# The first products of a two-layer decoder trunk: unnormed tokens, constant transposes ahead, and two widths in turn

## The chip, the cores and the metric

The kernel runs as one program on one core of one Trainium2 chip. The metric is the device time of one execution in microseconds. Engines are named as in the profile: PE is TensorE (PEld its weight loads), DVE is VectorE, ACT is ScalarE, POOL is GpSimd, SP is SyncE, which here only issues DMAs.

## The reference

The input x is one batch of 256 tokens by 1024 channels in float32. Two layers each do three steps: half a SwiGLU, a mixer, half a SwiGLU.

```python
def rms_norm(x, g):
    y = xf * lax.rsqrt(jnp.mean(xf * xf, axis=-1, keepdims=True) + EPS)
    return (y * g).astype(x.dtype)

def swiglu(h, w_gate, w_up, w_down):
    return (jax.nn.silu(h @ w_gate) * (h @ w_up)) @ w_down

for layer in range(2):
    x = x + 0.5 * swiglu(rms_norm(x, pre_norm[layer]), pre_w_gate[layer], pre_w_up[layer], pre_w_down[layer])
    h = rms_norm(x, mix_norm[layer])
    x = x + mixer(h)          # layer 0: SSD and MLA heads; layer 1: window attention and GLA heads
    x = x + 0.5 * swiglu(rms_norm(x, post_norm[layer]), post_w_gate[layer], post_w_up[layer], post_w_down[layer])
```

The hidden width of a SwiGLU is 2816, that is 22 blocks of 128. The change touches the four SwiGLU steps (called `ffn`) and the start of the program.

## The kernel before

**Two parts for each number.** Every float32 operand of a product is split in a high part (`wh`, `hT` at index 0, `acth`) and a low part (`wl`, index 1, `actl`). ACT casts the high part, DVE subtracts it from the source to get the low part. A product of two operands is then three products on PE: high by high, low by high, high by low.

**Weights.** `Stream.load` takes pieces of the packed weights in the order of use. Each piece (128 by 1024, 512 KB) is one DMA on SP's queue (line 73), one ACT cast (line 77) and one DVE subtraction (line 78). There are four raw buffers and eight pairs of `wh` and `wl`, so SP waits for DVE to free a raw buffer, and ACT and DVE wait for PE to free a pair.

**Norm.** `norm` squares and sums a tile of 128 tokens on ACT (line 245), takes the power −1/2 on POOL (line 229), multiplies by the factor and the gain on DVE (line 253, the tile `h`), transposes the eight 128 by 128 blocks on PE (`m_nrm`, line 117), and splits them into `hT` (lines 224 and 225). `hT` is four tiles, each with two of the eight channel blocks k, both parts and both token tiles t.

**A SwiGLU.** The first `G0` = 4 of the 22 blocks go with tokens as rows: `in_tok` (lines 272 to 274) makes 24 products of 512 columns for the gate (`p_g`) of token tile 0, 24 for up (`p_u`) of tile 0, then the same for tile 1; each pair is evicted (lines 359 and 360) and turned back by four transposes (`m_ffT`). The other 18 blocks f go with channels as rows: `in_ch2` makes, for each k, one product of 512 columns (`wh` by both parts of both token tiles, line 300) and one of 256 columns (`wl` by the high part, line 301). The down products (`proj`, lines 316 to 318) follow.

**The start.** x of tile 0 goes on SP's queue ahead of the weights, the gain on ACT's, the constants (`sq`, which holds the identity for the transposes) and x of tile 1 on POOL's. The other constants come in `constants_more`, on POOL's queue too, from 17 us on.

**The order of the work.** The program is not run in the order of the code: a scheduler places the instructions of each engine in a list by a timeline of its own, and each engine then works through its list from the front, waiting at each instruction for what that one needs. What is changed in the code can so move rows on every engine.

Of the kernel before, what the change touches and what calls it, by code (L numbers as in the profile page):

```python
# [15 lines left out]
P = 128  # L16
# [40 lines left out]
class Stream:  # L57
# [10 lines left out]
    def load(self, widths):  # L68
        nc = self.nc
        res = []  # L70
        for i, x in enumerate(widths):
            raw = self.pool.tile([P, x], F32, tag="raw", name=f"raw{self.n}_{i}", bufs=self.raw_bufs)
            nc.sync.dma_start(out=raw, in_=self.flat[self.off:self.off + P * x].rearrange("(p w) -> p w", w=x))
# [10 lines left out]
class Net:  # L84
# [38 lines left out]


    POOLS = {"a": (("a4", 4096, 9),), "b": (("b1", 1024, 2), ("b2", 2048, 4), ("b4", 4096, 13))}

    def constants(self):
        nc, a = self.nc, self.args
        self.sq = self.sb.tile([P, 3 * P], F32, tag="sq", name="sq", bufs=1)
        nc.gpsimd.dma_start(out=self.sq, in_=a["sq"])  # L130
        self.ident = self.sq[:, SQ["ident"]]
        self.mhalf = self.small([P, 8], "mhalf")
        nc.gpsimd.memset(self.mhalf, -0.5)

    def constants_more(self):
        nc, a = self.nc, self.args
        self.row = self.sb.tile([P, ROW_N], F32, tag="row", name="row", bufs=1)
        nc.gpsimd.dma_start(out=self.row, in_=a["row"].partition_broadcast(P))
        self.conv = self.small([P, 16, 5], "conv")
        nc.gpsimd.dma_start(out=self.conv, in_=a["conv"])  # L140
        kq = self.small([96, 2], "kq")
        nc.gpsimd.dma_start(out=kq, in_=a["kq"])
        self.wg = self.small([17, 256], "wg")
        nc.gpsimd.dma_start(out=self.wg, in_=a["wg"])
        self.pcol = self.small([P, 2], "pcol", I32)
        nc.gpsimd.dma_start(out=self.pcol, in_=a["pos_col"])
        self.prow = self.blk([P, S], "prow", I32)
        nc.gpsimd.dma_start(out=self.prow, in_=a["pos"].partition_broadcast(P))
# [11 lines left out]
        nc.gpsimd.dma_start(out=out_, in_=a["outside"])  # L160
# [78 lines left out]
    def norm(self, x, t, g, hT):  # L239

        nc = self.nc
        ss = self.small([P, 4], "ss", bufs=2)
        junk = self.small([P, 512], "junk")
        for h in range(2):
            nc.scalar.activation(out=junk, in_=x[:, h * 512:(h + 1) * 512], func=AF.Square, scale=1.0 / 32,
                                 accum_out=ss[:, h:h + 1])
        nc.vector.tensor_scalar(out=ss[:, 2:3], in0=ss[:, 0:1], scalar1=ss[:, 1:2], scalar2=EPS, op0=ALU.add, op1=ALU.add)  # L247
        self.power(ss[:, 3:4], ss[:, 2:3])
        h_ = self.blk([P, D], "h")
        turned = []  # L250
        for h in range(2):
            s = slice(h * 512, (h + 1) * 512)
            nc.vector.scalar_tensor_tensor(out=h_[:, s], in0=x[:, s], scalar=ss[:, 3:4], in1=g[:, s], op0=ALU.mult, op1=ALU.mult)
# [10 lines left out]
    def mm_tok(self, out, at, ks, t, w, first, last):  # L264

        mm = self.nc.tensor.matmul
        c = slice(t * P, (t + 1) * P)
        for i, k in enumerate(ks):
            ah, al = at(k)
            ah, al = ah[:, c], al[:, c]  # L270
            wh, wl = w[i]
            mm(out, ah, wh, start=first and i == 0, stop=False)  # L272
            mm(out, al, wh, start=False, stop=False)  # L273
            mm(out, ah, wl, start=False, stop=last and i == len(ks) - 1)  # L274

    def in_tok(self, out, hT, t, w, n, per):

        for s, (hi, lo) in enumerate(w):
            ww = [(hi[:, j * n:(j + 1) * n], lo[:, j * n:(j + 1) * n]) for j in range(per)]
            self.mm_tok(out, lambda k: self.hk(hT, k), range(per * s, per * s + per), t, ww, s == 0, s == len(w) - 1)  # L280
# [12 lines left out]
    def in_ch2(self, out, hT, w):  # L293
# [54 lines left out]
    def ffn(self, hT, x, after):  # L348
# [3 lines left out]
        wg = [s for _ in range(2) for s in st.load([2 * n0, 2 * n0])]  # L352
        wu = [s for _ in range(2) for s in st.load([2 * n0, 2 * n0])]
        for t in range(2):
            pg, pu = self.bank([P, n0], "g"), self.bank([P, n0], "u")
            self.in_tok(pg, hT, t, wg, n0, 2)
            self.in_tok(pu, hT, t, wu, n0, 2)
            sg = self.blk([P, n0], "sg")
            nc.scalar.activation(out=sg, in_=pg, func=AF.Silu)
            nc.vector.tensor_tensor(out=sg, in0=sg, in1=pu, op=ALU.mult)  # L360
# [95 lines left out]
    def mixer0(self, hT, x, after):  # L456
# [53 lines left out]
        for t in range(2):  # L510
            qn = self.blk([P, 8, 96], "qnat", grp="a")
            qr = self.blk([P, 8, 2, 16], "qr")
            for j in range(2):
                b = self.bank([P, 4, 96], "qb")
                bf = b.rearrange("p a b -> p (a b)")
                for k in range(3):
                    self.mm_tok(bf, lambda k: (qaT[0][:, k, :], qaT[1][:, k, :]), [k], t,
# [18 lines left out]
        for t in range(2):  # L536
            if t == 1:
                xbc(13, BC[1][:, 1, :])
# [4 lines left out]
            for j in range(2):  # L543
                b = self.bank([P, 4, P], "kvb")
                bf = b.rearrange("p a b -> p (a b)")
                for k in range(2):
                    self.mm_tok(bf, lambda k: (kvT[:, 0, k, :], kvT[:, 1, k, :]), [k], t,
# [458 lines left out]
    def run(self, out, steps):  # L1006
        nc = self.nc
        x = [self.big.tile([P, D], F32, tag=f"x{t}", name=f"x{t}", bufs=1) for t in range(2)]
        nc.sync.dma_start(out=x[0], in_=self.args["x"][:P, :])
        g, hT = self.gain(steps[0][1], nc.scalar), self.new_hT()  # L1010
        self.constants()
        self.norm(x[0], 0, g, hT)
        with self.tc.issue_after(self.pow.ins):
            nc.gpsimd.dma_start(out=x[1], in_=self.args["x"][P:, :])
        self.norm(x[1], 1, g, hT)
        with self.tc.issue_after(self.pow.ins):
            self.constants_more()
        for i, (what, _) in enumerate(steps):
            hT = self.step(what, hT, x, steps[i + 1][1] if i + 1 < len(steps) else None, out)

# [131 lines left out]
```

## Time and profile before

| | |
|---|---|
| median of 3 runs | 1045.36 us (1044.97 to 1046.19) |
| the profiled execution's own time | 1044.57 us |
| its span | 1042.8 us |
| PE busy | 1017.3 us (98%), 5561 instructions |
| DVE busy | 686.2 us (66%) |
| ACT busy | 570.3 us (55%) |
| mean granted TensorE clock | 0.995 |

The span runs from the first instruction to the last; the execution's own time is 1.8 us longer. A matmul's recorded time overlaps that of the next, so the pitch of the products is read from start to start. PE is nearly always at work; what an edit is worth is read from whether PE starts earlier, waits somewhere, or has more or slower products.

### The profile page before, as it was taken

The numbers are of one execution on the slowest core, as the hardware profiler recorded it, in microseconds if no ns is written. First come the engines' busy times: TensorE is split into PE (matmuls) and PEld (weight loads), VectorE is DVE, ScalarE is ACT, GpSimd is POOL, SyncE is SP. The second block draws the span as 40 slices with busy tenths as digits, with TensorE's granted clock in tenths as the row PEclk, the third lists the DMA queues.
The fourth block names the chain that finished last, engine by engine and source line by source line (L and its number), as shares of the span: only waits on it lengthen the run. The fifth ranks groups of instructions, "written<-read, shape, count | busy, mean of one in ns | idle before, by whom it ended". The sixth has DMA issues, their size and how long they took to land.

```text
span 1042.8 us, 15030 instructions
## 1 busy us (share of the span) xinstructions
PE 1017.3 (98%) x5561; PEld 872.3 (84%) x5561; DVE 686.2 (66%) x1054; ACT 570.3 (55%) x1036; POOL 87.5 (8%) x110
## 2 busy tenths in 40 slices
PE   6999999989799999999999999999999999999998
PEld 5888888988798888888888888888887778888886
DVE  6876754588777567677545767654588576666541
ACT  5755543467857366655434655643465456555530
POOL 2200000106233200000000000000011200000000
PEclk9999999999999999999999999999999999999999
DMA  8866555364434457565564655555463345665451
GB/s 300 280 204 188 191 190 176 115 209 162 151 111 161 144 182 241 184 198 184 197 190 159 223 197 186 191 189 168 142 222 101 102 160 181 191 193 184 148 197 40
DMA packets 52089, 185.93 MB, mean 178 GB/s; under 512 B 5911, under 2 KB 5928, under 8 KB 52016
## 3 DMA queue, kind: packets, MB, share of 16 engines
q1 hardware_dynamic: 49248, 176.58, 52.1%
q0 software_dynamic: 2048, 6.83, 2.0%
q10 hardware_dynamic: 720, 1.57, 0.4%
q8 instruction: 43, 0.70, 0.3%
q14 instruction: 30, 0.25, 0.1%
HBM read 183.89 MB, written 1.06 MB: 177 GB/s over the span
## 4 chain that ended last, share of the span: by engine, by line
PE 95%; ACT 1%; DVE 1%; DMA 1%; issue 1%; POOL 0%; DVEq 0%; ACTq 0%; POOLq 0%
PE p_u L300 13%; PE p_g L300 13%; PE p_acc L316 9%; PE p_acc L318 9%; PE p_acc L317 9%; PE p_u L301 7%; PE p_g L301 7%; PE p_g L272 1%; PE p_g L273 1%; PE p_g L274 1%; PE p_u L274 1%; PE p_u L272 1%; PE p_u L273 1%; PE p_xbc L289 1%; PE p_xbc L290 1%; PE p_xbc L291 1%
## 5 line engine op out<-in xcount | busy, mean ns | idle before, releaser
L78 DVE TENSOR_TENSOR wl<-raw,wh 128x1024 fp32r<-128x1024 f32 (+3 forms) x341 | 413.0, 1222 | 220.7 <-ACT wh L77 219.1
L77 ACT CAST wh<-raw 128x1024 fp32r<-128x1024 f32 (+3 forms) x341 | 351.8, 1038 | 306.1 <-PE p_acc L317 101.7
L300 PE MATMUL p_u<-hT,wh 128*128 128x512 f32 x576 | 204.1, 393 | 0.0
L300 PE MATMUL p_g<-hT,wh 128*128 128x512 f32 x576 | 204.0, 393 | 0.0
L301 PE MATMUL p_u<-hT,wl 128*128 128x256 f32 x576 | 161.7, 281 | 0.0
L301 PE MATMUL p_g<-hT,wl 128*128 128x256 f32 x576 | 161.5, 280 | 0.0
L318 PE MATMUL p_acc<-wl,acth 128*128 128x512 f32 x352 | 137.1, 389 | 0.0
L317 PE MATMUL p_acc<-wh,actl 128*128 128x512 f32 x352 | 137.0, 389 | 0.0
L316 PE MATMUL p_acc<-wh,acth 128*128 128x512 f32 x352 | 136.2, 391 | 0.0
L300 PEld LDWEIGHTS p_g<-hT,wh 128*128 128x128 f32 x576 | 107.9, 187 | 24.5
L300 PEld LDWEIGHTS p_u<-hT,wh 128*128 128x128 f32 x576 | 107.9, 187 | 24.4
L301 PEld LDWEIGHTS p_g<-hT,wl 128*128 128x128 f32 x576 | 108.9, 189 | 0.2
L301 PEld LDWEIGHTS p_u<-hT,wl 128*128 128x128 f32 x576 | 108.9, 189 | 0.0
L318 PEld LDWEIGHTS p_acc<-wl,acth 128*128 128x128 f32 x352 | 66.1, 188 | 13.8
L316 PEld LDWEIGHTS p_acc<-wh,acth 128*128 128x128 f32 x352 | 66.1, 188 | 13.6
L317 PEld LDWEIGHTS p_acc<-wh,actl 128*128 128x128 f32 x352 | 66.1, 188 | 13.4
L229 POOL TENSOR_TENSOR ss<-ss,mhalf 128x1 f32<-128x1 f32 x12 | 6.7, 557 | 577.5 <-DVE ss L247 577.5
L324 DVE SCALAR_TENSOR_TENSOR x<-p_acc,x 128x512 f32<-128x512 f32 x24 | 16.2, 688 | 36.4 <-PE p_acc L318 36.4
L289 PE MATMUL p_xbc<-hT,wh 128*128 128x256 f32 x128 | 38.2, 299 | 0.4 <-DVE cv L439 0.4
L290 PE MATMUL p_xbc<-hT,wh 128*128 128x256 f32 x128 | 37.8, 295 | 0.0
L291 PE MATMUL p_xbc<-hT,wl 128*128 128x256 f32 x128 | 37.6, 294 | 0.0
L376 DVE TENSOR_TENSOR sg<-sg 128x256 f32<-128x256 f32 x72 | 30.6, 426 | 7.9 <-DVE sg L373 0.9
(370 smaller groups left out, 1530.7 us busy)
## 6 DMA issues: line engine op xcount, KB each, us to landing
raw<-in_w SPq DMA_DIRECT2D x326, 512.0 KB, 4.3
gain<-in_gains POOLq DMA_DIRECT2D x5, 512.0 KB, 5.8
E<-acs_rows POOLq DMA_DIRECT2D x4, 512.0 KB, 6.2
raw<-in_w SPq DMA_DIRECT2D x4, 400.0 KB, 3.2
raw<-in_w SPq DMA_DIRECT2D x4, 288.0 KB, 2.8
raw<-in_w SPq DMA_DIRECT2D x3, 384.0 KB, 4.0
raw<-in_w SPq DMA_DIRECT2D x4, 272.0 KB, 2.9
out<-x ACTq DMA_DIRECT2D x4, 256.0 KB, 2.0
```

What stands on the lines that cost most here:

```text
L77: nc.scalar.copy(out=hi, in_=raw)
L78: nc.vector.tensor_tensor(out=lo, in0=raw, in1=hi.bitcast(F32), op=ALU.subtract)
L272: mm(out, ah, wh, start=first and i == 0, stop=False)
L289: mm(out, hi[:, cs], xh, start=k == 0, stop=False)
L290: mm(out, hi[:, cs], xl, start=False, stop=False)
L291: mm(out, lo[:, cs], xh, start=False, stop=k == KT - 1)
L300: mm(out, hi[:, cs], hT[k // 2][:, k % 2], start=k == 0, stop=k == KT - 1, skip_group_check=True)
L301: mm(out[:, 0, :], lo[:, cs], self.hk(hT, k)[0], start=False, stop=k == KT - 1, skip_group_check=True)
L316: first = nc.tensor.matmul(o, ah, w[0][:, s], start=k == 0, stop=False)
L317: nc.tensor.matmul(o, al, w[0][:, s], start=False, stop=False)
L318: nc.tensor.matmul(o, ah, w[1][:, s], start=False, stop=k == nk - 1)
L376: nc.vector.tensor_tensor(out=sg, in0=sg, in1=v[:, 1, :], op=ALU.mult)
```

## The change

Four things are changed.

1. The first SwiGLU does not wait for the norm. Both token tiles of x are transposed as they are, each channel is multiplied by its gain (`gained`, a DVE product with the column `gcol`), and the result `xT` is split. The factor of the norm, one number per token, is applied at the eviction, as the scale of the silu and in the product with up. The gate of both token tiles stands ahead of up. `hT` is still made for the 18 other blocks, by `normed`, after the first eight weight pieces are on the queue.
2. The identity is made on POOL (a memset and an affine select) and not read from memory. PE transposes it ten times ahead of x and eight times after x of tile 0.
3. x of tile 0 comes in two halves at the head of SP's queue, x of tile 1 behind two weight pieces, the gain behind eight, and the other constants behind 14, all on SP's queue.
4. `in_ch2` makes all eight products of 512 columns of a bank, then all eight of 256. That holds for all four SwiGLU steps, 144 banks.

The core of the diff:

```diff
     def constants(self):
-        nc.gpsimd.dma_start(out=self.sq, in_=a["sq"])
+        self.gcol = self.small([P, KT], "gcol")
+        nc.scalar.dma_start(out=self.gcol, in_=a["gain_col"])
         self.ident = self.sq[:, SQ["ident"]]
+        nc.gpsimd.memset(self.ident, 1.0)
+        nc.gpsimd.affine_select(out=self.ident, in_=self.ident, pattern=[[-1, P]], compare_op=ALU.is_equal, fill=0.0,
+                                base=0, channel_multiplier=1)
...
     def constants_more(self):
-        nc.gpsimd.dma_start(out=self.row, in_=a["row"].partition_broadcast(P))
+        nc.sync.dma_start(out=self.sq[:, P:], in_=a["sq"][:, P:])
+        nc.sync.dma_start(out=self.row, in_=a["row"].partition_broadcast(P))
...
+    def gained(self, x, run=None):
+        xT = [self.blk([P, 2, 4, P], f"xT{h}", F32R) for h in range(2)]
+        for h in range(2):
+            tp = self.tbank([P, 4, P], "nrm")
+            for j in range(4):
+                i = self.transpose(tp[:, j, :], x[:, h * 512 + j * P:h * 512 + (j + 1) * P])
+                if run:
+                    run.append(i)
+            v = self.blk([P, 4, P], "xg")
+            self.nc.vector.tensor_tensor(out=v, in0=tp, in1=self.gcol[:, 4 * h:4 * h + 4].unsqueeze(2).broadcast_to([P, 4, P]), op=ALU.mult)
+            last = self.split(xT[h][:, 0], xT[h][:, 1], v)
+        return lambda k: (xT[k // 4][:, 0, k % 4, :], xT[k // 4][:, 1, k % 4, :]), last
...
     def in_ch2(self, out, hT, w):
         for k in range(KT):
-            cs = slice(k * P, (k + 1) * P)
-            mm(out, hi[:, cs], hT[k // 2][:, k % 2], start=k == 0, stop=k == KT - 1, skip_group_check=True)
-            mm(out[:, 0, :], lo[:, cs], self.hk(hT, k)[0], start=False, stop=k == KT - 1, skip_group_check=True)
+            mm(out, hi[:, k * P:(k + 1) * P], hT[k // 2][:, k % 2], start=k == 0, stop=k == KT - 1, skip_group_check=True)
+        for k in range(KT):
+            mm(out[:, 0, :], lo[:, k * P:(k + 1) * P], self.hk(hT, k)[0], start=False, stop=k == KT - 1, skip_group_check=True)
...
     def ffn(self, hT, x, after):
-        wg = [s for _ in range(2) for s in st.load([2 * n0, 2 * n0])]
+        wg = st.load([2 * n0, 2 * n0])
+        self.now("first")
+        wg += st.load([2 * n0, 2 * n0])
         wu = [s for _ in range(2) for s in st.load([2 * n0, 2 * n0])]
...
+            if early:
+                nc.scalar.activation(out=sg, in_=pg, func=AF.Silu, scale=self.rs[t])
+                nc.vector.scalar_tensor_tensor(out=sg, in0=pu, scalar=self.rs[t], in1=sg, op0=ALU.mult, op1=ALU.mult)
...
+        for t, n, w in ((0, "g", wg), (1, "g", wg), (0, "u", wu), (1, "u", wu)) if early else \
+                ((0, "g", wg), (0, "u", wu), (1, "g", wg), (1, "u", wu)):
+            b[t, n] = self.bank([P, n0], n)
+            run = self.in_tok(b[t, n], hT, t, w, n0, 2, early and early[t])
+            if early:
+                if len(b) > 1:
+                    self.order(run[0], last)
+                last = run[-1]
+                self.between.pop("one", lambda _: None)(run[5])
+            elif n == "u":
+                evict(t)
+        self.now("all")
+        self.early = None
+        if early:
+            evict(0), evict(1)
         for f in range(G0, NF):
             w = st.load([D, D])
+            if f == G0 + 2:
+                self.now("more")
...
     def run(self, out, steps):
-        nc.sync.dma_start(out=x[0], in_=self.args["x"][:P, :])
-        g, hT = self.gain(steps[0][1], nc.scalar), self.new_hT()
+        for h in range(2):
+            nc.sync.dma_start(out=x[0][:, h * 512:(h + 1) * 512], in_=self.args["x"][:P, h * 512:(h + 1) * 512])
         self.constants()
-        self.norm(x[0], 0, g, hT)
+        hT = self.new_hT()
+        warm = self.sbank([P, 4, P], "warm", "a")
+        run = [self.transpose(warm[:, i % 4, :], self.ident) for i in range(10)]
+        self.early = {0: self.gained(x[0], run)[0]}
+        run += [self.transpose(warm[:, i % 4, :], self.ident) for i in range(8)]
+        self.in_turn(run)
...
+        def normed():
+            g = self.gain(steps[0][1], nc.sync)
+            for t in range(2):
+                self.norm(x[t], t, g, hT, rs[t])
+        self.between = {"first": second, "one": turned, "all": normed, "more": self.constants_more}
```

**PE at the start.** The list of PE from its first work on, before; `m_nrm` are the transposes of the normed tile 0.

```order
L117 MATMUL m_nrm_91<-sq,h_89 128x128 x4
L117 MATMUL m_nrm_101<-sq,h_89 128x128 x4
L272 MATMUL p_g_284<-wh_0_238,hT_2_75 128x512
L273 MATMUL p_g_284<-wh_0_238,hT_2_75 128x512
L274 MATMUL p_g_284<-wl_0_239,hT_2_75 128x512
```

And with the change, where `m_warm` are the transposes of the identity, `m_nrm_98` and `m_nrm_107` those of x of tile 0, `m_nrm_216` and `m_nrm_225` those of x of tile 1:

```order
L117 MATMUL m_warm_85<-sq 128x128 x10
L117 MATMUL m_nrm_98<-sq,x_70 128x128 x4
L117 MATMUL m_nrm_107<-sq,x_70 128x128 x4
L117 MATMUL m_warm_85<-sq 128x128 x8
L305 MATMUL p_g_189<-wh_0_142,xT_8_96 128x512
L306 MATMUL p_g_189<-wh_0_142,xT_8_96 128x512
...
L305 MATMUL p_g_189<-wh_1_148,xT_8_96 128x512
L306 MATMUL p_g_189<-wh_1_148,xT_8_96 128x512
L117 MATMUL m_nrm_216<-sq,x_71 128x128 x4
L117 MATMUL m_nrm_225<-sq,x_71 128x128 x4
```

The first products now read `xT`, and the transposes of tile 1 stand behind the eighth of them.

**PE where the first four blocks end.** Before, the last product of up of tile 1 and the first ones of block f = 4:

```order
L273 MATMUL p_u_345<-wh_1_280,hT_5_78 128x512
L274 MATMUL p_u_345<-wl_1_281,hT_5_78 128x512
L300 MATMUL p_g_417<-hT_2_75,wh_0_406 128x512
L301 MATMUL p_g_417<-hT_2_75,wl_0_407 128x256
L300 MATMUL p_g_417<-hT_2_75,wh_0_406 128x512
```

And with the change, where `h_323` and `h_344` are the normed tiles 0 and 1 that `normed` makes:

```order
L307 MATMUL p_u_296<-wl_1_186,xT_32_215 128x512
L117 MATMUL m_nrm_325<-sq,h_323 128x128
L117 MATMUL m_nrm_335<-sq,h_323 128x128 x4
L117 MATMUL m_ffT_368<-sq,sg_365 128x128 x4
L117 MATMUL m_ffT_378<-sq,sg_375 128x128 x4
L117 MATMUL m_nrm_346<-sq,h_344 128x128 x4
L117 MATMUL m_nrm_356<-sq,h_344 128x128 x4
L339 MATMUL p_g_398<-hT_3_81,wh_0_387 128x512 x2
```

Between the last product of up and the first of block 4 there now stand 21 transposes, the last eight of which turn `h_344`.

**DVE at the same place.** Before, around the eviction of up of tile 1 (`sg_394`):

```order
L225 TENSOR_TENSOR actl_48_230<-m_ffT_337,acth_42_224 128x4x128
L360 TENSOR_TENSOR sg_394<-sg_394,p_u_345 128x512
L78 TENSOR_TENSOR wl_1_578<-raw_1_575,wh_1_577 128x1024
L196 SCALAR_TENSOR_TENSOR rp_r_163<-rp_kl_166,rp_r_163 128x32
L196 SCALAR_TENSOR_TENSOR rp_r_163<-rp_kh_165,rp_r_163 128x32
L78 TENSOR_TENSOR wl_0_627<-raw_0_624,wh_0_626 128x1024
```

With the change, from the eviction of up of tile 1 (`sg_375`) on; `rp_` tiles belong to the table of rotations, `hT_3` to `hT_6` are the four tiles of `hT`, and the left-out rows are more of the `rp_` kind:

```order
L403 SCALAR_TENSOR_TENSOR sg_375<-p_u_296,ss_240,sg_375 128x512
L200 TENSOR_SCALAR rp_k_534<-rp_r_533 128x32
L235 TENSOR_TENSOR hT_3_81<-m_nrm_325,hT_3_81 128x2x128
...
L78 TENSOR_TENSOR wl_0_636<-raw_0_633,wh_0_635 128x1024
...
L235 TENSOR_TENSOR actl_24_134<-m_ffT_368,acth_18_128 128x4x128
L235 TENSOR_TENSOR hT_4_82<-m_nrm_325,hT_4_82 128x2x128
L235 TENSOR_TENSOR hT_5_83<-m_nrm_335,hT_5_83 128x2x128
L235 TENSOR_TENSOR actl_24_134<-m_ffT_378,acth_18_128 128x4x128
...
L78 TENSOR_TENSOR wl_1_642<-raw_1_639,wh_1_641 128x1024
L273 SCALAR_TENSOR_TENSOR h_344<-x_71,ss_240,gain_44_321 128x512 x2
...
L235 TENSOR_TENSOR hT_3_81<-m_nrm_346,hT_3_81 128x2x128
```

The multiplication that makes `h_344` stands 13 rows behind the eviction, and the split of tile 1 into `hT_3`, which the first product of block 4 reads, five rows behind that.

## Rows read from the trace of the kernel before

**Rows 1.** The page: the chain that ended last, by engine.

```profile
PE 95%; ACT 1%; DVE 1%; DMA 1%; issue 1%; POOL 0%; DVEq 0%; ACTq 0%; POOLq 0%
```

**Rows 2.** Timeline of the start: start us, us, engine, line, operation, tiles, [idle before].

```profile
5.99 0.63 ACT L245 ACTIVATE junk<-x 128x512 f32<-128x512 f32 x1 [3.53 <-DMA x<-in_x]
...
7.99 1.04 ACT L77 CAST wh<-raw 128x1024 fp32r<-128x1024 f32 x1
...
9.27 1.97 PE L117 MATMUL m_nrm<-sq,h 128*128 128x128 f32 x8 [9.27 <-DVE h L253]
...
10.89 0.78 PE L272 MATMUL p_g<-wh,hT 128*128 128x512 f32 x1
...
11.99 0.63 PE L274 MATMUL p_g<-wl,hT 128*128 128x512 f32 x1
...
12.42 0.63 PE L272 MATMUL p_g<-wh,hT 128*128 128x512 f32 x1
...
15.61 0.40 PE L274 MATMUL p_g<-wl,hT 128*128 128x512 f32 x1
```

**Rows 3.** DMA of the first 30 us: GB/s in 40 slices; issues, KB, us to landing.

```profile
GB/s 0 0 66 98 399 393 355 354 406 415 415 415 431 426 410 382 235 180 300 202 289 393 328 300 262 333 329 270 278 203 289 388 240 344 410 404 426 306 197 115
...
gain<-in_gains ACTq DMA_DIRECT2D x1, 512.0 KB, 5.5
...
out<-in_outside POOLq DMA_DIRECT2D x1, 128.0 KB, 6.0
```

**Rows 4.** Windows, PE alone: us, busy (x), granted clock, DMA share, GB/s.

```profile
223.20:226.90 3.70, 3.70 (x19) 0.55 0.63 211
...
285.20:288.40 3.20, 3.13 (x14) 0.50 0.58 179
```

**Rows 5.** Timeline of PE where the first four blocks end.

```profile
36.04 0.39 PE L274 MATMUL p_u<-wl,hT 128*128 128x512 f32 x1
36.27 0.39 PE L300 MATMUL p_g<-hT,wh 128*128 128x512 f32 x1
```

**Rows 6.** Groups of VectorE lines in 0 to 60 us: busy us, mean ns.

```profile
L78 DVE TENSOR_TENSOR wl<-raw,wh 128x1024 fp32r<-128x1024 f32 x23 | 28.1, 1232 | 3.4 <-ACT wh L77 3.3
...
L225 DVE TENSOR_TENSOR hT<-m_nrm,hT 128x256 fp32r<-128x256 f32 x8 | 3.2, 417 | 0.0
...
L253 DVE SCALAR_TENSOR_TENSOR h<-x,ss,gain 128x512 f32<-128x512 f32 x4 | 2.8, 747 | 1.4 <-POOL ss L229 1.4
...
L225 DVE TENSOR_TENSOR actl<-m_ffT,acth 128x512 fp32r<-128x512 f32 x2 | 1.4, 684 | 0.0
...
L196 DVE SCALAR_TENSOR_TENSOR rp_r<-rp_kl,rp_r 128x32 f32<-128x32 f32 x6 | 1.4, 230 | 0.0
```

**Rows 7.** Groups of ScalarE lines in 0 to 60 us: busy us, mean ns.

```profile
L77 ACT CAST wh<-raw 128x1024 fp32r<-128x1024 f32 x24 | 25.1, 1051 | 12.3 <-DMA raw<-in_w 8.5 <-PE p_u L300 1.9 <-PE p_g L300 1.8
...
L224 ACT CAST acth<-m_ffT 128x512 fp32r<-128x512 f32 x2 | 1.2, 580 | 0.0
```

**Rows 8.** Timeline of PE after an idle stretch in the first mixer.

```profile
283.80 1.12 PE L117 MATMUL m_pT<-sq,p 128*128 128x128 f32 x4 [5.33 <-POOL p L415]
```

**Rows 9.** Timeline of PE: gate and up, the down products, and one width of 256.

```profile
60.05 0.39 PE L300 MATMUL p_g<-hT,wh 128*128 128x512 f32 x1
...
71.49 0.39 PE L300 MATMUL p_g<-hT,wh 128*128 128x512 f32 x1
...
189.97 0.39 PE L317 MATMUL p_acc<-wh,actl 128*128 128x512 f32 x1
...
193.60 0.39 PE L318 MATMUL p_acc<-wl,acth 128*128 128x512 f32 x1
...
213.98 0.28 PE L289 MATMUL p_xbc<-hT,wh 128*128 128x256 f32 x1
...
219.61 0.28 PE L291 MATMUL p_xbc<-hT,wl 128*128 128x256 f32 x1
```

**Rows 10.** Timeline of GpSimd: its first arithmetic.

```profile
7.87 0.56 POOL L229 TENSOR_TENSOR ss<-ss,mhalf 128x1 f32<-128x1 f32 x1 [5.74 <-DVE ss L247]
```

More of the change, by code (lines that the diff above doesn't have):

```diff
@@ L122, in order, with in_turn @@
                                mybir.DependencyInfo(mybir.DependencyClass.NoSync, mybir.DependencyReason.DATA), reason="order")
+    def in_turn(self, run):
+        for a, b in zip(run, run[1:]):
+            self.order(b, a)
     POOLS = {"a": (("a4", 4096, 9),), "b": (("b1", 1024, 2), ("b2", 2048, 4), ("b4", 4096, 13))}
@@ L262, in norm, with mm_tok, in_tok @@
         return turned
[L264 removed]
+    def gained(self, x, run=None):
[10 more added lines that the diff above has]
+        return lambda k: (xT[k // 4][:, 0, k % 4, :], xT[k // 4][:, 1, k % 4, :]), last
+    def mm_tok(self, out, at, ks, w, first, last):
         mm = self.nc.tensor.matmul
[L267 removed]
+        run = []
         for i, k in enumerate(ks):
             ah, al = at(k)
[L270 removed]
             wh, wl = w[i]
[L272 to L276, printed above, removed]
+            run += [mm(out, ah, wh, start=first and i == 0, stop=False),
+                    mm(out, al, wh, start=False, stop=False),
+                    mm(out, ah, wl, start=False, stop=last and i == len(ks) - 1)]
+        return run
+    def in_tok(self, out, hT, t, w, n, per, at=None):
+        c = slice(t * P, (t + 1) * P)
+        if at is None:
+            at = lambda k: tuple(a[:, c] for a in self.hk(hT, k))
+        run = []
         for s, (hi, lo) in enumerate(w):
             ww = [(hi[:, j * n:(j + 1) * n], lo[:, j * n:(j + 1) * n]) for j in range(per)]
[L280 removed]
+            run += self.mm_tok(out, at, range(per * s, per * s + per), ww, s == 0, s == len(w) - 1)
+        return run
     def in_ch(self, out, hT, w):
@@ L536, in mixer0 @@
         for t in range(2):
+            c = slice(t * P, (t + 1) * P)
             if t == 1:
@@ L1008, in run, with second, turned, now @@
         x = [self.big.tile([P, D], F32, tag=f"x{t}", name=f"x{t}", bufs=1) for t in range(2)]
-        nc.sync.dma_start(out=x[0], in_=self.args["x"][:P, :])
-        g, hT = self.gain(steps[0][1], nc.scalar), self.new_hT()
+        for h in range(2):
+            nc.sync.dma_start(out=x[0][:, h * 512:(h + 1) * 512], in_=self.args["x"][:P, h * 512:(h + 1) * 512])
         self.constants()
-        self.norm(x[0], 0, g, hT)
[L1013 to L1017, printed above, removed]
+        hT = self.new_hT()
[4 more added lines that the diff above has]
+        self.in_turn(run)
+        rs = []
+        def second():
+            nc.sync.dma_start(out=x[1], in_=self.args["x"][P:, :])
+        def turned(behind):
+            run = [behind]
+            self.early[1], last = self.gained(x[1], run)
+            self.in_turn(run)
+            for t in range(2):
+                rs.append(self.rms(x[t], last))
+            self.rs = rs
+        def normed():
+            g = self.gain(steps[0][1], nc.sync)
+            for t in range(2):
+                self.norm(x[t], t, g, hT, rs[t])
+        self.between = {"first": second, "one": turned, "all": normed, "more": self.constants_more}
         for i, (what, _) in enumerate(steps):
             hT = self.step(what, hT, x, steps[i + 1][1] if i + 1 < len(steps) else None, out)
+    def now(self, where):
+        with self.tc.issue_after(self.st.dma.ins):
+            self.between.pop(where, lambda: None)()
     def step(self, what, hT, x, following, out):
```

52 lines of the change are left out of this document (31 added, 21 removed).

## The prediction

> **What bounds the kernel now.** The chain of waits comes first: TensorE carries 95% of the path to the end [rows 1], so the time changes by what TensorE gains or loses in three places: the start, the point where the first four blocks end, and the pitch of the products. The timeline of the start shows x there at 5.99 us, where the first square on ACT begins, the transposes at 9.27, the first product at 10.89, and products 0.43 us apart from 11.99 to 12.42 [rows 2]. [...] The DMA view, 40 slices of 0.75 us, shows about 400 GB/s once the transfers run, and the gain, 512 KB, landing 5.5 us after its issue, so it travels beside x [rows 3]. The granted clock is 0.50 and 0.55 in two later stretches, 3.2 and 3.7 us long [rows 4]. Where the first four blocks end, the last product starts at 36.04 and block 4 at 36.27: no wait there [rows 5].
>
> **The start.** The gain no longer travels beside x: 512 KB at some 400 GB/s is 1.28 us, so x is there near 4.7 and the first weight piece 1.28 us later, near 6.0. Four transposes and the product with the gain (like h, 0.75 us) give the two halves of `xg` near 6.4 and 7.1 [rows 6]. ACT's list has the cast of the weights first, 1.05 us, to 7.05, and then that of half a tile, 0.58 us as for `acth`: first product near 7.7 [rows 7]. DVE makes `wl` first, 1.23 us from 7.1, then the low part of `xT`, 0.68: second product near 9.0. That is 2.5 us ahead of before, which got its second just ahead of the one at 11.99.
>
> It isn't kept. Six products on (at 0.43 us, to 12.0) stand the eight transposes of tile 1, at the lower clock some 1.7 us (those of before stood at 9.27, the product behind them at 10.89). Before, the rise came about 4.5 us after the first product. After 283.80, where the engine had been idle for 5.33 us, transposes ran first and the rise came only at 288.40 [rows 8, 4]. I take it that transposes do little for the clock, and that it rises some 3.8 us after the products go on at 13.7, at 17.5: 9 more products by then at 0.427, and the other 79 of 96 at 0.2265, 17.9 us, to 35.4. With three transposes (0.3) and small waits (0.5) block 4 could start at 36.2, against 36.27 before: **−0.1 us**. Bounds: −3.7 if the constant transposes bring the clock up before the first product (17 slow products then cost 0.2 us less each, 3.4, and the transposes of tile 1 some 0.3 less), +1.0 if the constants that now share SP's queue delay the weights by most of a piece (1.28).
>
> [...] No row here shows transposes alone for long enough to tell.
>
> **The wait ahead of block 4.** Block 4 reads `hT`, which now is made late. In the order of DVE the normed tile 1, `h_344`, stands behind the eviction of the last up. From that product's end T on, DVE does: the drain and eviction, 0.2 + 0.68 (like `actl`, same shape); three splits of `hT`, 3 × 0.417; two `wl`, 2 × 1.232; two `actl`, 2 × 0.684; six small operations of the rotation table at about 0.2, 1.3; and the two halves of `h_344`, 2 × 0.747 [rows 6]. Sum 0.88 + 1.25 + 2.46 + 1.37 + 1.3 + 1.49 = 8.75 us. Behind them, before the low half of `hT_3` of tile 1 is there: one more split, three small operations and that split itself, 0.42 + 0.6 + 0.42 = 1.45. The transposes and casts run beside these. So block 4 starts 10.2 us after T instead of 0.23: **+10.0 us**. TensorE has 13 transposes to do until `h_344` comes, some 1.5 us, and idles for over 6. Nothing else covers it: its list is fixed and the waiting transposes stand ahead of all products of block 4. Below, the term is 8.7, if the small operations are as short as 0.1 us; above, 11.9, if a `wl` more waits for its raw piece ahead of `h_344`. `h_344` could have run much sooner by its data (x of tile 1 and its factor); it is the place in the list that costs.
>
> **The clock behind it.** After 5.33 us idle TensorE worked at granted clock 0.50 for 3.2 us, and at 0.55 in another such stretch of 3.7 [rows 4, 8]. A stretch of that kind now stands at the head of block 4: half of 3.2 to 0.45 of 3.7, **+1.7 us** (1.6 to 1.9). In exchange, four of the transposes back (`m_ffT`) that before stood behind the start of block 4 lie in the wait: 4 × 0.1, **−0.4**.
>
> **512 and 256 apart.** 144 banks of 8 pairs are 1152 pairs. The pair now has a pitch of (71.49 − 60.05)/33 = 346.7 ns. Products of 512 alone: (193.60 − 189.97)/16 = 226.9; of 256 alone: (219.61 − 213.98)/47 = 119.8; sum 346.7 [rows 9]. So **0.0 us**. Both rows carry a weight load for each product, as here. Bounds from the resolution of 10 ns at each end: some ±0.6 ns a pair, −0.7 to +0.7 us. A far end: 256 at half of the 512's pitch, 113.4, which makes −6.4 ns × 1152 = −7.4; I give it little, since 119.8 is the row of the very shape.
>
> **Sum.** −0.1 + 10.0 + 1.7 − 0.4 + 0.0 = +11.2. On the profiled execution's own time, 1044.57 (its span is 1.8 shorter), that is 1055.8; the median of the runs is 0.8 above it, so 1056.5 us. Adding the lower ends, −3.7 + 8.7 + 1.6 − 0.4 − 0.7 = +5.5, gives 1050.9; the upper, 1.0 + 11.9 + 1.9 − 0.3 + 0.7 = +15.2, gives 1060.6.
>
> **Rivals.**
>
> *The constant transposes do lift the clock.* Then the products run at the upper level from the first: −3.7 at the start, of which late constants on SP's queue (their casts on ACT stand ahead of the first cast of `hT`; each landed 4.5 to 6 us after its issue, `outside` 6.0 [rows 3]) give back some 1: 1053.7 us. For it: at 283.80 the idle time ended with transposes and the rise came 4.6 us on. Against it: counted from the products, about 3.1 us. 0.17.
>
> *The identity is late.* The trace of before shows no memset or affine select; GpSimd's first arithmetic stands at 7.87, after 5.74 idle [rows 10]. If the identity is there only at about 8.4, all transposes move from 4.7 to 8.4; the weights' cast is then done before, and the first product comes near 11, 3.3 later than 7.7. The wait behind the first blocks stays: 1059.8 us. 0.12.
>
> *The other side: a fixed cost of a product that a change of width sets.* The line through 226.9 at 512 and 119.8 at 256 columns leaves 12.7 ns at no columns. Were that the price of switching, or hidden within a run of one width, the regrouped pair would save 2 × 12.7 = 25.4 ns, × 1152 = −29.3 us, against +11.2: 1027.3 us. It decides from 11.2/1152 = 9.7 ns saved a pair. Against it: the rows of one width alone already carry the 12.7 ns [rows 9]. 0.06.
>
> [...]
>
> *Nothing in sum.* The far end of the 256 (−7.4) together with the lifted clock (−3.7) cancels the wait: 1056.5 − 11.1 = 1045.4. 0.05.
>
> **How the numbers follow.** Forecast 0.60 (its own range 1054 to 1059), lifted clock 0.17, late identity 0.12, other side 0.06, nothing 0.05. Taking in the first three cases with the bounds gives 1050.5 to 1061, with 0.11 and a little of the edges outside. A difference under 0.2%, 2.1 us, cannot be told from none. Faster 0.06, same 0.05, slower 0.89.
>
> **What would show it.** In the changed kernel's timeline: first product near 7.7; TensorE idle for 6 us or more, ended by DVE's `h` (line 273), then a few us at half the clock, with block 4 (line 339) starting some 10 us after the last up; the eight pairs of a bank still 346.7 ns each. The forecast is wrong if that wait is under 5 us, if a pair has become shorter by several ns, or if the first four blocks end earlier than 33 us.

## The result and the profile after

The changed kernel takes 1059.36 us (median of 4 runs, 1057.50 to 1061.63), the kernel before in the same comparison 1045.16. The ratio is 1.0138, 95% interval 1.0121 to 1.0155: 14.2 us slower. The forecast was 1056.5 with a range of 1050.5 to 1061.0; direction and place were right, the loss was forecast 3 us too small. Three executions of 1.7 to 5.8 ms, two of e1_norm_early and one of e10_before_grouped, are left out of the medians below.

The profiled run is the slowest of the four (1061.63, 17.1 above the profiled run before), so pieces are read from it and not the sum. Its chain of waits by engine, against [rows 1], rows of the timeline of its start, against [rows 2, 10], and two windows of TensorE, against [rows 4] (the granted clock is the number behind the busy time):

```profile
PE 90%; DMA 4%; DVE 2%; ACT 2%; issue 1%; POOL 0%; SPq 0%; ACTq 0%; DVEq 0%
```

```profile
0.80 0.20 POOL L138 MEMSET sq<- 128x128 f32 x1 [0.29 <-POOLq L1238]
...
1.26 0.30 POOL L139 TENSOR_SCALAR_AFFINE_SELECT sq<-sq 128x128 f32<-128x128 f32 x1
...
1.61 2.39 PE L117 MATMUL m_warm<-sq 128*128 128x128 f32 x10 [1.61 <-POOL sq L139]
...
3.81 1.72 PE L117 MATMUL m_nrm<-sq,x 128*128 128x128 f32 x8
...
5.37 1.04 PE L117 MATMUL m_warm<-sq 128*128 128x128 f32 x8
...
7.87 1.04 ACT L77 CAST wh<-raw 128x1024 fp32r<-128x1024 f32 x1 [5.04 <-DMA raw<-in_w]
...
9.48 0.79 PE L305 MATMUL p_g<-wh,xT 128*128 128x512 f32 x1 [3.08 <-ACT xT L234]
...
11.41 0.63 PE L307 MATMUL p_g<-wl,xT 128*128 128x512 f32 x1
...
15.77 0.39 PE L305 MATMUL p_g<-wh,xT 128*128 128x512 f32 x1
```

```profile
5.14:8.56 3.42, 1.27 (x12) 1.00 0.90 292
8.60:15.30 6.70, 5.27 (x15) 0.50 0.86 308
```

GpSimd has the identity at about 1.6 us (a memset of 0.20 and a select of 0.30). The eight transposes of x, from 3.81 to 5.37, take 0.2 us each, the eight of the identity behind them 1.04 us in all: the clock went up at about 5.14 us, where the trace's record of it begins, before any product. Then TensorE waits 3.08 us for the cast of `xT`, which stands on ACT behind that of the first weights (7.87), and its first product, 9.48, and those from 11.41 on run at the lower clock again (0.43 us from start to start). At 15.77 one takes 0.39: the clock is up again, in the trace's record from 15.4 to 42.7. The first product is 1.4 us earlier than before, and no more.

The place where the first four blocks end, against [rows 5], in TensorE's timeline:

```profile
36.18 0.39 PE L307 MATMUL p_u<-wl,xT 128*128 128x512 f32 x1
...
41.24 0.66 PE L117 MATMUL m_ffT<-sq,sg 128*128 128x128 f32 x4 [3.68 <-DVE sg L403]
...
48.02 2.08 PE L117 MATMUL m_nrm<-sq,h 128*128 128x128 f32 x8 [6.12 <-DVE h L273]
...
50.03 1.22 PE L339 MATMUL p_g<-hT,wh 128*128 128x512 f32 x2
```

The last up product starts at 36.18 (36.04 before), block 4 at 50.03 (36.27 before): 13.85 us where there were 0.23. TensorE is idle for 3.68 us, ended by the eviction `sg`, and for 6.12, ended by `h`. DVE's timeline in that stretch has the cause; its durations answer to [rows 6]:

```profile
38.02 0.23 DVE L835 TENSOR_TENSOR gg<-row 128x64 f32<-128x64 f32 x1 [1.61 <-DMA row<-in_row]
...
38.65 1.23 DVE L78 TENSOR_TENSOR wl<-raw,wh 128x1024 fp32r<-128x1024 f32 x1
...
39.79 0.73 DVE L196 TENSOR_SCALAR rp_r<-row,pf 128x16 f32<-128x16 f32 x2
...
40.44 0.74 DVE L403 SCALAR_TENSOR_TENSOR sg<-p_u,ss,sg 128x512 f32<-128x512 f32 x1
...
42.68 1.23 DVE L78 TENSOR_TENSOR wl<-raw,wh 128x1024 fp32r<-128x1024 f32 x1 [0.60 <-ACT wh L77]
...
47.13 1.41 DVE L273 SCALAR_TENSOR_TENSOR h<-x,ss,gain 128x512 f32<-128x512 f32 x2
...
49.55 0.42 DVE L235 TENSOR_TENSOR hT<-m_nrm,hT 128x256 fp32r<-128x256 f32 x1
```

The last eviction could start at 36.6 by its data and starts at 40.44: DVE waits 1.61 us for `row`, one of the constants that now go through SP's queue, and has four small operations, a `wl` and two operations on the angles (0.73) ahead of it. From there the list runs as the order shows it: `h` at 47.13, 6.7 us behind the eviction, and the low half of `hT` that block 4 waits for at 49.55. The windows of TensorE behind that stretch and in the first mixer, against [rows 4]:

```profile
50.05:52.90 2.85, 2.85 (x8) 0.50 0.02 7
...
237.30:244.00 6.70, 4.69 (x22) 0.50 0.61 207
```

The clock is at half until 52.9, which costs 1.4 us. In the first mixer the stretch at half clock is 6.8 us long here and 3.4 before (223.56 to 226.97).

From the start of block 4 to the first down product it is 101.93 us, against 100.40 before: 1.5 more. The 1.4 of clock and 0.7 for this step's 288 pairs, which take 349.1 ns and not 346.7 (below), less some 0.4 for the four transposes back that now lie in the wait, would be 1.7. Grouped by width, the products look like this in TensorE's timeline, against [rows 9]; eight products to a row:

```profile
70.95 2.00 PE L339 MATMUL p_u<-hT,wh 128*128 128x512 f32 x8
72.79 1.12 PE L341 MATMUL p_u<-hT,wl 128*128 128x256 f32 x8
...
82.12 2.00 PE L339 MATMUL p_u<-hT,wh 128*128 128x512 f32 x8
```

Four banks in 11.17 us are 349.1 ns a pair, in all four SwiGLU steps. Before, three steps have 346.7, and the fourth has 353.1, in this piece of it (two banks, that is sixteen pairs, in 5.65 us):

```profile
889.79 0.40 PE L300 MATMUL p_g<-hT,wh 128*128 128x512 f32 x1
...
895.44 0.40 PE L300 MATMUL p_g<-hT,wh 128*128 128x512 f32 x1
```

### The profile page after: what moved, and what is told of

It is laid out like the page before. It is cut to its first block, busy times and chain, and to the rows that moved or that the text cites. A ratio compares the mean times of both kernels' runs of the same rounds, so it can differ in the third digit from the quotient of the medians.

```text
span 1059.9 us, 15047 instructions
## 1 busy us (share of the span) xinstructions
PE 1027.4 (97%) x5595; PEld 880.6 (83%) x5595; DVE 691.4 (65%) x1062; ACT 577.3 (54%) x1043; POOL 82.1 (8%) x103
## 4 chain that ended last, share of the span: by engine, by line
PE 90%; DMA 4%; DVE 2%; ACT 2%; issue 1%; POOL 0%; SPq 0%; ACTq 0%; DVEq 0%
PE p_g L339 13%; PE p_u L339 13%; PE p_acc L356 9%; PE p_acc L358 9%; PE p_acc L357 9%; PE p_g L341 6%; PE p_u L341 6%; DMA raw<-in_w 2%; PE p_g L306 1%; PE p_g L305 1%; PE p_g L307 1%; DVE wl L78 1%; PE p_u L307 1%; PE p_u L305 1%; PE p_u L306 1%; PE m_nrm L117 1%
## 5 line engine op out<-in xcount | busy, mean ns | idle before, releaser
L339 PE MATMUL p_g<-hT,wh 128*128 128x512 f32 x576 | 146.1, 394 | 0.0
L339 PE MATMUL p_u<-hT,wh 128*128 128x512 f32 x576 | 145.7, 393 | 0.0
L339 PEld LDWEIGHTS p_g<-hT,wh 128*128 128x128 f32 x576 | 104.2, 190 | 19.1 <-DVE hT L235 0.3
L339 PEld LDWEIGHTS p_u<-hT,wh 128*128 128x128 f32 x576 | 104.1, 190 | 18.7
L341 PEld LDWEIGHTS p_u<-hT,wl 128*128 128x128 f32 x576 | 78.7, 190 | 5.6
L341 PEld LDWEIGHTS p_g<-hT,wl 128*128 128x128 f32 x576 | 78.6, 190 | 5.6
L341 PE MATMUL p_u<-hT,wl 128*128 128x256 f32 x576 | 81.0, 283 | 0.0
L341 PE MATMUL p_g<-hT,wl 128*128 128x256 f32 x576 | 80.3, 282 | 0.0
```

Source lines behind the costliest of these rows:

```text
L339: mm(out, hi[:, k * P:(k + 1) * P], hT[k // 2][:, k % 2], start=k == 0, stop=k == KT - 1, skip_group_check=True)
L341: mm(out[:, 0, :], lo[:, k * P:(k + 1) * P], self.hk(hT, k)[0], start=False, stop=k == KT - 1, skip_group_check=True)
```

## The experiments

Theory A, mine: the loss is what block 4 waits for, `h` of tile 1 at a late place of DVE's list, and the clock that falls meanwhile. Theory B: the constants on SP's queue, which hold the last eviction, set the wait. A third question is what the regrouping and the early clock do. "Wait" is from the start of the last up product to that of block 4, in the profiled run.

**e1_norm_early.** `normed` is called right behind the gate of both tiles:

```diff
                 self.between.pop("one", lambda _: None)(run[5])
+                if (t, n) == (1, "g"):
+                    self.now("all")
```

> The normed tiles are called for right behind the gate products, so that h of tile 1 stands ahead of the last eviction in DVE's list; the constants stay where they are. Theory A (block 4 waits because h of tile 1 stands late in DVE's list): the wait from the last up product to block 4 falls from 13.6 us to about 7, since the eviction is still held by the constants; time near 1052. Theory B (the constants on SP's queue alone set the wait): it stays within 2 us of 13.6, time 1057 to 1061.

1054.10 us, ratio 1.0084 (1.0070 to 1.0099): 5.3 less than the changed kernel. The wait is 7.54 us. In its DVE timeline the constants still come between, but `h` is ahead of the eviction; the window is TensorE's:

```profile
35.10 1.41 DVE L273 SCALAR_TENSOR_TENSOR h<-x,ss,gain 128x512 f32<-128x512 f32 x2
...
40.67 0.74 DVE L403 SCALAR_TENSOR_TENSOR sg<-p_u,ss,sg 128x512 f32<-128x512 f32 x1
...
43.17 0.41 DVE L235 TENSOR_TENSOR hT<-m_nrm,hT 128x256 fp32r<-128x256 f32 x1
```

```profile
43.64:48.95 5.31, 5.31 (x13) 0.50 0.72 236
```

Behind the eviction at 40.67 there are 3 us left and not 9.6. B alone is out, and the 7 us that A forecast came; the time is 2.1 us above its number. Part of that is the clock: it is at half for the first 5.3 us of block 4, which costs 2.7 us where the changed kernel lost 1.4.

**e2_const_later.** The constants six blocks later:

```diff
-            if f == G0 + 2:
+            if f == G0 + 8:
                 self.now("more")
```

> The constants are loaded six blocks later, behind 26 weight pieces; h of tile 1 stays behind the eviction. Theory A: the eviction runs at once (0.9 us), but h still stands behind it, behind one wl, two actl and three hT; block 4 about 7.5 us after the last up product instead of 13.6, the clock still falls; time near 1053. Theory B: the wait falls under 3 us and the time to about 1046.

1056.28 us, ratio 1.0100 (1.0084 to 1.0116): 3.1 less. Wait 10.48, where A said 7.5 and B under 3. The eviction did not run at once, as its DVE timeline shows:

```profile
35.80 2.47 DVE L78 TENSOR_TENSOR wl<-raw,wh 128x1024 fp32r<-128x1024 f32 x2
38.81 1.23 DVE L78 TENSOR_TENSOR wl<-raw,wh 128x1024 fp32r<-128x1024 f32 x1 [0.54 <-ACT wh L77]
39.95 0.74 DVE L403 SCALAR_TENSOR_TENSOR sg<-p_u,ss,sg 128x512 f32<-128x512 f32 x1
```

With the constants gone, three `wl` of blocks 6 and 7 stand ahead of the eviction in the list, and the last of them waits for its cast. What held the eviction was not only the constants but whatever stood ahead of it.

**e3_both.** The two edits above together.

> Both edits, h early and constants later. Theory A with both parts of the wait: block 4 some 3.6 us after the last up product (eviction 0.9, one wl behind its cast to 2.5, one actl, one hT), too short for the clock to fall: 10.0 us of wait and 1.5 us of clock less, near 1048. If something else holds block 4, the time stays above 1053.

1056.75 us, ratio 1.0106 (1.0093 to 1.0119). Wait 7.30, not 3.6: my number failed. Nor does any run show that a wait of 3.6 us is too short for the clock to fall: in the changed kernel it fell at the start in one of 3.08 us. The eviction starts at 40.91, behind `h`, a split of `hT` and the same three `wl`, in its DVE timeline:

```profile
37.07 1.22 DVE L78 TENSOR_TENSOR wl<-raw,wh 128x1024 fp32r<-128x1024 f32 x1
38.20 0.42 DVE L235 TENSOR_TENSOR hT<-m_nrm,hT 128x256 fp32r<-128x256 f32 x1
38.54 2.46 DVE L78 TENSOR_TENSOR wl<-raw,wh 128x1024 fp32r<-128x1024 f32 x2
40.91 0.75 DVE L403 SCALAR_TENSOR_TENSOR sg<-p_u,ss,sg 128x512 f32<-128x512 f32 x1
```

So the two savings don't add: 6.3 us by one edit, 3.4 by the other, 6.6 by both. The wait is the longest way through one list, and each edit only changes what stands in front. That its median is 2.7 us above that of e1, with a wait no longer, is not settled; in its profile the first mixer takes 2.7 us more than in e1's, with 6.8 us at half clock against 3.4.

**e4_pairs_back.** Only the products of a bank in turns again:

```diff
-        for k in range(KT):
-            mm(out, hi[:, k * P:(k + 1) * P], hT[k // 2][:, k % 2], start=k == 0, stop=k == KT - 1, skip_group_check=True)
-        for k in range(KT):
-            mm(out[:, 0, :], lo[:, k * P:(k + 1) * P], self.hk(hT, k)[0], start=False, stop=k == KT - 1, skip_group_check=True)
+        for k in range(KT):
+            cs = slice(k * P, (k + 1) * P)
+            mm(out, hi[:, cs], hT[k // 2][:, k % 2], start=k == 0, stop=k == KT - 1, skip_group_check=True)
+            mm(out[:, 0, :], lo[:, cs], self.hk(hT, k)[0], start=False, stop=k == KT - 1, skip_group_check=True)
```

> Only the order of products of 512 and 256 in a bank is put back to turns of one and one. By the prediction: no change within 1 us (0.0 a pair), 1058 to 1061. Rival (grouping by width costs some 2 ns a pair, as three of the four SwiGLU steps of the changed kernel's trace seem to show): 0.5 to 2.4 us less, 1057 to 1059. Other rival (grouping saves 25 ns a pair): 29 us more.

1060.55 us, ratio 1.0148 (1.0135 to 1.0161), against 1.0138 (1.0121 to 1.0155): no difference that can be told.

**e10_before_grouped.** The other way round: the kernel before with nothing but the regrouping (the diff of e4 with + and − exchanged).

> The kernel before with nothing but the regrouping: eight products of 512, then eight of 256. From the pitches in the traces (346.6 ns a pair before in three SwiGLU steps and 353 in the fourth, 349.2 in all four of the changed kernel) +0.7 us in three steps and -1.1 in the fourth: +1 us, 1045 to 1047, hardly told from no change. By the prediction: 0.0, within 0.7. Rival (grouping saves 25 ns a pair): 1016.

1045.23 us, ratio 1.0008 (0.9995 to 1.0020): the same. The regrouping neither saves 25 ns a pair nor costs anything that counts. Its start is that of the kernel before, but in TensorE's timeline the clock is up earlier than in [rows 2]:

```profile
12.71 0.40 PE L273 MATMUL p_g<-wh,hT 128*128 128x512 f32 x1
```

**e5_no_wait.** `hT` made before up ends. Its core, beside e2's line and the gain loaded behind four weight pieces:

```diff
+                if (t, n) == (1, "g"):
+                    self.now("all")
+                if n == "u":
+                    for i in self.turned[t]:
+                        self.order(run[14], i)
...
-            evict(0), evict(1)
+            evict(0)
...
+            if early and f == G0:
+                evict(1)
```

> hT is made before the last up ends: gain behind four weight pieces, normed right behind the gate products, the transposes of h of tile 1 in the middle of up of tile 1, the eviction of tile 1 behind block 4, constants six blocks later. Theory A (all of the loss lies in what block 4 waits for, and in the clock that falls in that wait): block 4 starts within 2 us of the last up product, the clock stays up, 13.6 + 1.5 us less than the changed kernel, some of it (1 to 3 us) paid again in waits inside up: 1045 to 1048. Rival (the weights for block 4 are late whatever the norm does, since gate of both tiles ahead of up frees the pairs of weights later): block 4 still waits 5 us or more, 1051 to 1056.

1051.93 us, ratio 1.0063 (1.0043 to 1.0083): 7.4 less than the changed kernel. In TensorE's timeline block 4 follows up as before, 0.23 us behind it:

```profile
37.14 0.63 PE L117 MATMUL m_nrm<-sq,h 128*128 128x128 f32 x4 [1.50 <-DVE hT L235]
...
39.67 0.39 PE L307 MATMUL p_u<-wl,xT 128*128 128x512 f32 x1
39.90 0.62 PE L339 MATMUL p_g<-hT,wh 128*128 128x512 f32 x2
```

But up ends at 39.67, 3.5 us later, since the transposes now wait inside it (0.53, 0.43 and 1.50 us), and the clock doesn't fall there (block 4's first two products take 0.45 us from 39.90, start to start). Its first down product is at 141.41 us, 10.6 ahead of the changed kernel's 151.96 and 4.7 behind the kernel before. A's mechanism came, but not its range of 1045 to 1048: it had 1 to 3 us for waits inside up, and up ended 3.5 us later than in the changed kernel. The work for `h` of tile 1 was moved, not taken away.

**e11_no_wait_pairs.** e5 with the diff of e4.

> e5_no_wait with the products in turns of one and one again. If grouping costs 2.6 ns a pair in three steps and saves 4 in the fourth: about 1 us less than e5_no_wait, 1049.5 to 1052. If it costs nothing: the same. All that then separates it from the kernel before is the wait inside up and the mixer.

1052.87 us, ratio 1.0082 (1.0060 to 1.0104), beside e5's 1.0063 (1.0043 to 1.0083): the same, not the 1 us less that I had read from the pitches. In its trace the pairs of the first step take 353 ns and not 346.7 (eight in 2.83 us, from 68.00 to 70.83), and the clock is at half from 39.5 to 42.8, inside up.

**e7_after_warm40.** More transposes of the identity:

```diff
-        run += [self.transpose(warm[:, i % 4, :], self.ident) for i in range(8)]
+        run += [self.transpose(warm[:, i % 4, :], self.ident) for i in range(40)]
```

> The changed kernel with 40 transposes of the identity behind x of tile 0 in place of 8, so that TensorE is not idle between 6.4 us and its first product at 9.5. If the rise at 5.14 us holds only while TensorE works: the first products run at the upper level, the last up product ends some 3 us sooner. If the wait ahead of block 4 is set by what DVE waits for (weights, constants, h), block 4 gains less than 1.5 of these 3 us and the time is 1058 to 1060; if it is set from the end of up, all 3: 1056.

1057.68 us (1057.35 to 1061.73), ratio 1.0133 (1.0111 to 1.0156): the same as the changed kernel. TensorE's timeline:

```profile
4.03 1.40 PE L117 MATMUL m_nrm<-sq,x 128*128 128x128 f32 x8
5.27 4.53 PE L117 MATMUL m_warm<-sq 128*128 128x128 f32 x40
9.55 0.48 PE L305 MATMUL p_g<-wh,xT 128*128 128x512 f32 x1
9.87 0.39 PE L306 MATMUL p_g<-wh,xT 128*128 128x512 f32 x1
10.10 0.40 PE L307 MATMUL p_g<-wl,xT 128*128 128x512 f32 x1
...
19.34 0.80 PE L305 MATMUL p_g<-wh,xT 128*128 128x512 f32 x1 [3.12 <-ACT xT L234]
```

The clock holds over the 40 transposes, and the first products are 0.23 us apart. It buys nothing: at 19.34 TensorE has waited 3.12 us for `xT` of tile 1, whose cast on ACT stands behind one of weights that had waited 1.22 us for its DMA; the clock falls (products 0.43 us apart from 21.27), and up ends later, at 38.76. Nor did the first product come sooner: the weights were there earlier in this run (cast from 6.42 on, not 7.87), but the 40 transposes held TensorE until 9.55. Block 4 starts at 48.98, 1.0 us sooner than in the changed kernel, though up ended 2.6 later.

**e8_no_const_turns.** No transposes of the identity at all:

```diff
-        run = [self.transpose(warm[:, i % 4, :], self.ident) for i in range(10)]
+        run = []
...
-        run += [self.transpose(warm[:, i % 4, :], self.ident) for i in range(8)]
```

> The changed kernel without its 18 transposes of the identity. If they lifted the clock at 5.14 us: no rise before the products, which begin near 9.5 as now; since in the changed kernel the clock had fallen again by 8.56, the products see no difference and the time is the same within 1 us, 1058 to 1060.5. If the time grows by more than 1.5 us, they did serve the products.

1059.03 us (1056.04 to 1059.85), ratio 1.0133 (1.0112 to 1.0154): the same. Up ended at 34.16, 2.0 us sooner than in the changed kernel (the clock came up at 12.9 us here, not at 15.4), and block 4 started at 49.19. Three kernels whose up ends at 34.2, 36.2 and 38.8 have block 4 at 49.2, 50.0 and 49.0: it does not follow the end of up but DVE's list.

**e6_before_warm50.** The early clock alone, in the kernel before:

```diff
-        nc.gpsimd.dma_start(out=self.sq, in_=a["sq"])
+        nc.gpsimd.memset(self.ident, 1.0)
+        nc.gpsimd.affine_select(out=self.ident, in_=self.ident, pattern=[[-1, P]], compare_op=ALU.is_equal, fill=0.0,
+                                base=0, channel_multiplier=1)
+        nc.gpsimd.dma_start(out=self.sq[:, P:], in_=a["sq"][:, P:])
...
+        warm = self.sbank([P, 4, P], "warm", "a")
+        run = [self.transpose(warm[:, i % 4, :], self.ident) for i in range(50)]
+        for i, j in zip(run, run[1:]):
+            self.order(j, i)
         self.norm(x[0], 0, g, hT)
```

> The kernel before, with nothing but the identity made on GpSimd and 50 transposes of it ahead of those of the normed tile. If transposes lift the clock (the changed kernel's clock rose at 5.14 us, before any product): it is at its upper level when the first product starts near 10.9, some 10 products take 0.23 instead of 0.43 us: 2.1 us less, and 0.5 from the transposes of tile 0; 1042.5 to 1043.5. If only products lift it: no change, 1045.

1047.79 us, ratio 1.0027 (1.0015 to 1.0038): slower, against both expectations. The clock did come up (the transposes of tile 0 take 1.23 us and not 1.97), but in TensorE's timeline the first product starts at 13.12 and the second at 15.12:

```profile
2.60 7.24 PE L117 MATMUL m_warm<-sq 128*128 128x128 f32 x50 [2.60 <-POOL sq L132]
9.67 1.23 PE L117 MATMUL m_nrm<-sq,h 128*128 128x128 f32 x8
13.12 0.49 PE L275 MATMUL p_g<-wh,hT 128*128 128x512 f32 x1 [2.22 <-ACT hT L227]
15.12 0.50 PE L276 MATMUL p_g<-wh,hT 128*128 128x512 f32 x1 [1.50 <-DVE hT L228]
```

The 50 transposes moved the order: four `wl` now stand ahead of the first split of `hT`, which ran at 14.65. Block 4 starts at 39.87, 3.6 us later than before.

**e9_warm_pinned.** The same, with the first casts and subtractions of weights held behind the splits, as in the kernel before:

```diff
+            if self.pins:
+                for late, soon in zip(both, self.pins.pop(0) or ()):
+                    self.order(late, soon)
...
+        self.st.pins = [None, self.four[0], self.four[2], None, self.four[3]]
```

> The kernel before with the identity on GpSimd and 50 transposes of it, as in e6_before_warm50, but the casts and subtractions of the first weights are held in the places that they have in the kernel before, so that no row of wl passes ahead of the first splits of hT. If e6 lost only by those rows: the clock is up when the first product starts near 10.7, about 10 products at 0.23 and not 0.43 us, block 4 begins some 2 us sooner, 1042.5 to 1043.5. Rival (the weights come no faster than the products of before took them): the gain is waited away again in the first 24 products, 1044.5 to 1046.

1044.47 us, ratio 0.9999 (0.9985 to 1.0013): no gain. The first product starts at 11.89 and the products run at the upper clock from the first, but they wait at 14.44 for a split of `hT` and at 20.86 for a `wl`, and block 4 starts at 37.16, 0.9 us later than before. TensorE's timeline of the start:

```profile
11.89 0.50 PE L280 MATMUL p_g<-wh,hT 128*128 128x512 f32 x1
...
12.69 0.40 PE L282 MATMUL p_g<-wl,hT 128*128 128x512 f32 x1
...
14.44 0.50 PE L281 MATMUL p_g<-wh,hT 128*128 128x512 f32 x1 [0.42 <-DVE hT L232]
...
20.86 0.50 PE L282 MATMUL p_u<-wl,hT 128*128 128x512 f32 x1 [0.43 <-DVE wl L79]
```

That is the rival's time, but the run does not settle why: the 50 transposes took until 10.83, and those of `h` behind them, which could have started at about 9.7 (0.8 us behind the start of `h`, 8.85, as before), waited for them. So the first product is 1.0 us later than before, mostly by the transposes' own time, and some 2 us that the clock gives go into waits. Whether an early clock without that delay would pay is open. No version here beats the kernel before.

## Why the prediction came out as it did

**The wait ahead of block 4: right in kind, too short by 3.6 us.** Forecast +10.0, measured 13.85 − 0.23 = +13.6. It lies outside the term's own bounds, 8.7 to 11.9. The step that failed is the first of its sum, "from that product's end T on, DVE does: the drain and eviction". DVE was not free at T: the eviction started at 40.44 and not at 36.6, 3.8 us late. From there to `h` the sum held: 6.7 us measured, where eviction and what stands between make 0.68 + 1.25 + 2.46 + 1.37 + 1.3, the 7.1 of the forecast; 2.9 from `h` to block 4, where it had 1.49 + 1.45. The 0.2 us of drain in that first step is an estimate that no run shows: the eviction's start was set by the rows ahead of it. A further 0.2 us is a slip: the sum counts from the product's end and then takes off 0.23 us that are counted from its start. I had the late constants as half of a rival about the start, at "some 1" us, and never asked which rows stand ahead of the eviction in DVE's list and when their data land. In the changed kernel they are rows that read the constants and a `wl`. But the constants alone did not make the eviction late: in e2, without them, it started at 39.95, still 3.2 us after it could, behind three `wl`. The 3.4 us that e2 saves lie mostly behind the eviction, where the rows of the rotation table and one `wl` are gone too: 6.9 us to block 4 and not 9.6. e1 shows the share of `h`: 6.3 shorter. e7 and e8 show that T was the wrong origin altogether.

The median lies inside the range, the profiled run, 1061.63, does not, and there is luck in that: the upper end of the range, 1061, holds 1.0 us for a late start that did not come, and it makes room for a wait above its bound.

**The start: −0.1 forecast, +0.1 measured, by two errors that cancel.** The first product came at 9.48 and not at 7.7. The first weights landed at 7.8 and not at 6.0 (6.1 us after their issue at 1.71; before, 6.8 us after 1.18), so their cast started at 7.87, as before (7.99, [rows 2]); from there to the first product it took 1.6 us, as forecast. Of the sixteen completions that the trace records for that transfer, fifteen had come by 6.1 us and the last at 7.8; in e7 all were there by 6.4. So the weights did come forward, but for the last part. And the clock was up at 15.4 and not at 17.5. That is partly luck: e10, with the start of the kernel before, has it up at 12.7, 1.9 us behind its first product, where the trace of before has 4.5. I had held, from two rises in the trace of before, that transposes do little for the clock. They lifted it: in the changed kernel it was up at 5.1 us with only transposes done, and in e7 it held through 40 more. In the traces of the changed kernel, e1, e2, e5, e6, e7, e9 and e11, all with transposes of the identity, the first rise comes between about 4.6 and 8.3 us by the pitch of the transposes (0.2 us below, 0.11 above), ahead of the first product; in e8, without those of the identity, at 12.9, behind it. The rise is lost in the wait of 3.08 us that follows, and e8 without them is as fast. So the rival "the constant transposes do lift the clock" was right in its mechanism and wrong in its price, 1053.7: in that trace there was nothing to keep the clock up for until the weights came, and where it was kept up, in e7, a later wait took the gain.

**The clock behind the wait: right.** +1.7 forecast, half clock from 50.03 to 52.9, 1.4 us. The −0.4 for the four transposes back was not measured by itself; they do lie in the wait, at 41.24. What I did not price is the first mixer, where the stretch at half clock was 6.8 us in the changed kernel's profile and 3.4 before. It changes from run to run and is not clearly the change's: 6.8 us in e3, e4 and e5, 3.4 in e1, e2, e7 and e11, none in e8 and, with the kernel before, none in e6. The four times of the changed kernel go with their mean granted clock: 0.985, 0.985, 0.989 and 0.990 for 1061.63, 1060.35, 1058.37 and 1057.50 us. How much of the remaining loss lies in it is open.

**Regrouping: right in sum, and partly by luck.** 0.0 forecast; e10 and e4 measure no change. But the pair did change: 349.1 ns grouped, where the forecast had 346.7 ± 0.6. In three steps that is 2.4 ns more, and in the fourth, which I had not read and which took 353 before, 4 less; the two nearly cancel. The fixed-cost rival (near 1027) is out: a pair takes 349 ns when grouped.

**Late identity: out.** It was there at 1.6 us. The prediction misread the trace of before here: that trace does show memsets on GpSimd, from 0.24 to 0.34 us and at 1.99, of 0.10 to 0.13 us each, and they spoke against this rival.

**What is left.** e5 removes the wait and the half clock behind it and is still 0.63% slower than before: in its profile about 3.6 us lie ahead of the end of up, 2.5 of them in waits of the transposes, 1.1 between there and the first down product, and 1.5 in the first mixer.

## What to carry to other kernels

When a change moves where something is made, ask for each engine that works through a fixed list what stands ahead of the row that makes it, and for each of those rows when its own data land; the wait is the longest way through that list, not a count from the moment the consumer is ready. Making a first product earlier, or the clock faster, was worth nothing here, where the next operands came no faster. Two edits that shorten ways through the same list need not add: 6.3 and 3.4 us gave 6.6.

## What the runs showed of the hardware

Transposes alone raised TensorE's clock here and held it: in the changed kernel it was up at 5.14 us, the first product at 9.48; in e7 the eight of x take 1.40 us, the 40 of the identity behind them 0.107 us each ((9.55 − 5.27)/40), and the products right behind those are 0.23 us apart.

In the changed kernel, in runs of eight and eight, the pair of 512 and 256 columns takes 349 ns in every SwiGLU step. In turns, in the kernel before, it takes 346.7 in three steps and 353 in the fourth, of the same code, and in e11 353 in the first step too; the cause is open.
